# Block sums of a product's weights: from vector instructions to accumulating transfers

## The chip, the cores and the metric

The kernel runs on one core of a Trainium2 chip. The metric is the device time of one execution in microseconds, the median of three runs. A profile is one further execution with the hardware profiler; its span is the time from the first instruction to the last, which is a little less than that execution's own time. All instructions are in one program with five engine queues: PE multiplies matrices, ACT applies functions and copies, DVE and POOL do elementwise work, SP issues transfers. POOL can issue transfers too, in its own queue.

## The reference, cut to what matters

One residual layer on x of 512 tokens by 1024 channels, in f32. After a normalisation, one wide projection gives the inputs of two attention mixers, of their gates and of two output gates:

```
h = rmsnorm(x, norm_g)
(q_lat, c_kv, k_rope, z_a, q_b, k_b, v_b, z_b,
 q_idx, k_idx, w_idx, gate_a, gate_b) = split(h @ w_in)
...
merged = sigmoid(gate_a) * (y_a @ w_o_a) + sigmoid(gate_b) * (y_b @ w_o_b)
x = x + merged @ w_out
return rmsnorm(x, final_g)
```

The change touches the part of `h @ w_in` that gives `v_b` (1024 to 512) and six of the eight 128-channel tiles of `gate_b` (1024 to 1024), and there only how the same products are formed.

## The kernel before, in words

**Three-fold products.** Every f32 operand is held as a rounded part and a remainder (`hi`, `lo`), and each product is three matmuls (`mm3`, issued at L390): hi by hi, hi by lo, lo by hi. A weight tile comes from DRAM by a transfer of SP (L417) into one of four load buffers (`raw`, 128 x 1024 f32). ACT copies it to `hi` (L292), and DVE (L318) or POOL (L320) subtracts to get `lo` (`lo_part`). So ACT and one of DVE and POOL each spend one instruction on every 128 x 512 of weights before PE can use it.

**Seven products for eight.** For `v_b` (`values2`) and for three pairs of gate tiles (`proj2`: tiles 0 and 1, 2 and 3, 4 and 5 of `gate_b`) the product is cut into two by two blocks and formed with seven block products in place of eight, in Winograd's manner. That needs four block sums on the weights' side of each, made in `prep`, four sums per input tile, made once in `input_sums`, and seven steps that collect the block products from PSUM, in `seven`. The first tile of a pair holds the blocks b11 and b21 in its buffer, the second b12 and b22. Before the change `prep` of a pair forms t3 = b22 - b12 in a slot of its own, then b12 - b11 over b12, t3 + b11 over b11, and b21 minus that over b21. Each is one elementwise instruction of 128 x 512 on DVE (L318) or POOL (L320). The block products are taken in the order 1, 6, 2, 7, 5, 4, 3. Products 1, 2, 4 multiply plain blocks of h (`s_h` in the profile), 6, 7, 5, 3 sums of them (`s_hs`). Each of a pair's seven is twelve matmuls of 256 columns; each of `v_b`'s is twenty-four. The bank of product 6 is read once and then has product 7 added into it.

**A planner sets the order.** The program is written as threads (generators), each yielding one step after another. When the kernel is built, `Flow.run` keeps a clock for each engine, prices each step by a written formula, always emits the step that can start first by these clocks (with small terms for priority), and, where a step may go to either of two engines, takes the one that it expects to finish sooner. The resulting order of each engine's instructions is fixed: on the chip every engine runs its list in order and waits where an operand isn't there. A changed price or a new step can therefore move instructions anywhere behind it. `soon(...)` marks steps for which POOL is offered at its plain price.

**Jobs.** The weight tiles are jobs in a fixed list. Around the change it reads: the four tiles of `v_b` (`VB`), `GB0 GB1`, `sb2` (a key and a query tile), `zb1`, `GB2 GB3`, `sb3`, `zb2`, `GB4 GB5`, a tile of `w_out`, `zb3` and so on. One thread (`fetcher`) loads them in that order as load buffers come free. One thread (`splitter`) prepares them in that order, and for `VB` and the pairs it runs the whole `prep` before it goes on to the next job; slots for split weights are limited (`PCAP` 10, `WCAP` 8). One thread (`multiplier`) emits their matmuls in that order. The attention heads are threads beside it and fill in between.

**Transfers from POOL.** `pool_dma` (L421) and `pool_dma_out` (L437) issue transfers from POOL's queue. Both are used in the first 75 us only: constants, the rotary tables, and eight copies for the indexer. The planner prices the issue at 1.03 us of POOL.

Of the kernel before, what the change touches and what calls it, by code (L numbers as in the profile page):

```python
# [14 lines left out]
ALU = mybir.AluOpType  # L15
# [227 lines left out]
def tile_block(ctx: ExitStack, tc: tile.TileContext, a: dict, out: bass.AP, bias_dram: bass.AP):  # L243
# [40 lines left out]
    def bufs(*vs):  # L284
        return [v.buf for v in vs if isinstance(v, View)]
# [24 lines left out]
    def soon(step):  # L310
        step.pbias = 0.0
        return step
# [86 lines left out]
    def cut(pair, sl):  # L399
        return pair[0][:, sl], pair[1][:, sl]  # L400
# [17 lines left out]

    def pool_dma(dst, src):
        s = src.ap if isinstance(src, View) else src  # L420
        step = Step([("POOL", 1.03, lambda: nc.gpsimd.dma_start(dst.ap, s))], bufs(dst), bufs(src))  # L421
        step.moves = 4.0 * dst.n * dst.ap.shape[0] / 360000
        yield step

    def act_dma(dst, src):
        step = Step([("ACT", 0.06, lambda: nc.scalar.dma_start(dst.ap, src))], bufs(dst), [])
# [7 lines left out]
        return View(v.buf, bass.AP(a.tensor, a.offset + (col[1] - 1) * col[0], [row, [-col[0], col[1]]]))  # L434

    def pool_dma_out(dst, src):
        step = Step([("POOL", 1.03, lambda: nc.gpsimd.dma_start(dst, src.ap))], [], bufs(src))  # L437
        step.moves = 4.0 * src.n * src.ap.shape[0] / 360000
        yield step

# [405 lines left out]
    def splitter():  # L846
        for job in jobs:
            yield Until(lambda: job.raw is not None)
            if job.prep:
                if job.body:  # L850
                    yield from job.prep(job)
                else:
                    spawn(job.prep(job), 9)
                continue
            for p, w in enumerate(job.widths):
                o = sum(job.widths[:p])
                yield from split_w(job.raw[:, o : o + w], w, job.parts, p, job.cls, job.cap, p == len(job.widths) - 1)

    def multiplier():
        for job in jobs:  # L860
# [23 lines left out]

    hs = {}

    def input_sums():

        yield Until(lambda: sums_due[0] in done)
        for k in range(4):
            f = []
            for i in (k, k + 4):
                t = yield slot("tmp", TCAP)
                yield soon(tt(t.all.f, hT[i][0].all.f, hT[i][1].all.f, ALU.add, BOTH))
                f.append(t)
            x, y = (t.all.f for t in f)
            yield soon(tt(x[:, HI], x[:, LO], x[:, HI], ALU.subtract, BOTH))
            yield soon(tt(y[:, HI], y[:, HI], x[:, HI], ALU.subtract, BOTH))  # L900
            yield soon(tt(x[:, LO], y[:, HI], x[:, LO], ALU.add, BOTH))
            yield soon(tt(y[:, LO], y[:, LO], y[:, HI], ALU.subtract, BOTH))
            for i in range(2):
                hi = yield slot("hs")
                lo = yield slot("hs")
                yield act(hi.all, f[i].all.f)
                yield soon(lo_part(lo.all, f[i].all.f, hi.all))
                put(f[i])
                hs[k, i] = (hi, lo)

    def side(n, k):

        if n in (1, 2, 4):
            return cut(hT[k if n == 1 else k + 4], HI if n == 4 else LO)
        return cut(hs[k, n in (3, 6)], HI if n in (6, 7) else LO)

    def proj2(first, second):

        parts, raws = {}, []

        def hold(job):
            raws.append(job.raw)
            yield Until(lambda: True)

        def split_t(n, x):
            hi = yield slot("w", PCAP)
            lo = yield slot("w", PCAP)
# [48 lines left out]
        Job(a[first[0]][first[1]], [512, 512], None, prep=hold)  # L976
        Job(a[second[0]][second[1]], [512, 512], body, prep=prep)

    def seven(times, part, c11, c21, c12, c22, end):

        sums = set()

        def take(key, step, release=None):
            yield step
            if release:
                put(release)
            sums.add(key)
            if len(sums) == 7:
                end()

        def add(dst, ps, y):
            return tt(dst, part(ps), y, ALU.add)
# [16 lines left out]
        spawn(take("c22", add(c22, z, c21)), 0)  # L1009
# [5 lines left out]
        spawn(take("c12", add(c12, z, c12), z), 0)  # L1015

    def pair_done():
        hT_done()
# [6 lines left out]
    def values2():  # L1025
# [18 lines left out]

        def prep(job):
            yield Until(lambda: len(raws) == 3)
            raws.append(job.raw)
            b11, b21, b12, b22 = ([r[:, :S], r[:, S:]] for r in raws)

            def op(dst, x, y, how):  # L1050
                for i in range(2):
                    yield soon(tt(dst[i], x[i], y[i], how, BOTH))

            yield from split_t(1, b11)
            t = []
            for _ in range(2):
                t.append((yield slot("wsum")))
            t3 = [x.all.f for x in t]
            yield from op(t3, b22, b12, ALU.subtract)
            yield from op(b12, b12, b11, ALU.subtract)  # L1060
            yield from op(b11, t3, b11, ALU.add)
            yield from split_t(6, b11)
            yield from split_t(2, b21)
            yield from split_t(7, t3)
            put(*t)
            yield from split_t(5, b12, raws[2])
            yield from op(b21, b21, b11, ALU.subtract)
            put(raws[0])
            yield from split_t(4, b21, raws[1])
            yield from split_t(3, b22, raws[3])  # L1070

        def times(n, ps, more=False):
            for k in range(4):
# [940 lines left out]
```

## Time and profile before

| what | value |
|---|---|
| median of three runs | 434.74 us (434.64 to 435.3) |
| the profiled execution's own time | 435.09 us |
| its span | 433.3 us |
| granted clock of PE | 0.996 |
| busy: PE, DVE, ACT, POOL | 420.7, 382.5, 263.1, 131.7 us |
| transfers | 66.28 MB, mean 153 GB/s |

The span leaves out 1.79 us of the execution's own time (435.09 - 433.3). A busy share is the time in which an engine had an instruction in work; matmuls overlap one another in the pipeline, so a PE that is always busy needn't run at its best rate. In a timeline a row gives start, duration, engine, line, operation, what is written and read, the shape, how many, and in brackets the idle time before it with what ended that. In the groups the columns are the count, the shortest, median and longest duration in ns, and the first and last start. Windows give the busy time of each engine within each stretch, with the number of instructions.

### The profile page before, as it was taken

The numbers are of one execution on the slowest core, as the hardware profiler recorded it, in microseconds if no ns is written. First come the engines' busy times: TensorE is split into PE (matmuls) and PEld (weight loads), VectorE is DVE, ScalarE is ACT, GpSimd is POOL, SyncE is SP. The second block draws the span as 40 slices with busy tenths as digits, with TensorE's granted clock in tenths as the row PEclk, the third lists the DMA queues.
The fourth block names the chain that finished last, engine by engine and source line by source line (L and its number), as shares of the span: only waits on it lengthen the run. The fifth ranks groups of instructions, "written<-read, shape, count | busy, mean of one in ns | idle before, by whom it ended". The sixth has DMA issues, their size and how long they took to land.

```text
span 433.3 us, 7175 instructions
## 1 busy us (share of the span) xinstructions
PE 420.7 (97%) x2303; PEld 364.6 (84%) x2303; DVE 382.5 (88%) x842; ACT 263.1 (61%) x590; POOL 131.7 (30%) x152
## 2 busy tenths in 40 slices
PE   8999999899999999999999999999999999999994
PEld 5899968789888888788899988998898888888883
DVE  4599599999999999999978898989699847999995
ACT  5985785746473556655655668585389524346624
POOL 2255877444556558720000001021010001001452
PEclk9999999999999999999999999999999999999998
DMA  8973335564517451184335424525342696528405
GB/s 257 393 236 108 75 109 179 127 199 104 159 50 194 129 145 48 52 240 134 98 86 195 147 97 107 131 86 199 88 146 74 240 342 220 191 102 290 147 2 194
DMA packets 30277, 66.28 MB, mean 153 GB/s; under 512 B 4648, under 2 KB 5176, under 8 KB 30240
## 3 DMA queue, kind: packets, MB, share of 16 engines
q1 hardware_dynamic: 29264, 64.34, 48.4%
q0 software_dynamic: 832, 1.35, 1.2%
q8 instruction: 18, 0.29, 0.3%
q14 instruction: 19, 0.16, 0.1%
q10 hardware_dynamic: 144, 0.13, 0.1%
HBM read 50.49 MB, written 4.21 MB: 126 GB/s over the span
## 4 chain that ended last, share of the span: by engine, by line
PE 51%; DVE 26%; issue 8%; ACT 5%; POOL 4%; DMA 4%; SPq 1%; POOLq 0%; DVEq 0%; ACTq 0%
PE ps L390 47%; DVE mask L789 3%; DVE sm L788 3%; PE ps L407 3%; DVE sm L1430 2%; DVE s_mg L318 2%; DVE s_wo L318 2%; ACT s_w L292 2%; DVE s_ph L318 1%; DMA raw<-w_kvl 1%; SPq L417 1%; DVE s_pair L318 1%; DVE s_wsum L318 1%; DMA s_op<-s_op 1%; ACT junk L301 1%
## 5 line engine op out<-in xcount | busy, mean ns | idle before, releaser
L390 PE MATMUL ps<-s_h,s_w 128*128 128x512 f32 (+1 forms) x732 | 169.1, 378 | 0.0
L390 PEld LDWEIGHTS ps<-s_h,s_w 128*128 128x128 f32 x732 | 128.5, 188 | 22.4 <-issue 0.3
L292 ACT CAST s_w<-raw 128x512 fp32r<-128x512 f32 (+3 forms) x124 | 71.2, 591 | 21.7 <-DVE raw L318 9.6
L320 POOL TENSOR_TENSOR s_w<-raw,s_w 128x512 fp32r<-128x512 f32 (+2 forms) x41 | 50.7, 1244 | 88.2 <-ACT s_w L292 70.5
L318 DVE TENSOR_TENSOR s_w<-raw,s_w 128x512 fp32r<-128x512 f32 (+2 forms) x83 | 55.1, 679 | 10.6 <-ACT s_w L292 9.2
L390 PE MATMUL ps<-s_ys,s_w 128*128 128x512 f32 x192 | 43.7, 389 | 0.0
L390 PEld LDWEIGHTS ps<-s_ys,s_w 128*128 128x128 f32 x192 | 36.0, 188 | 7.5
L390 PE MATMUL ps<-s_wo,s_mg 128*128 128x512 f32 (+1 forms) x156 | 33.0, 373 | 0.0
L390 PE MATMUL ps<-s_w,s_xg 128*128 128x328 f32 (+1 forms) x192 | 32.4, 323 | 0.0
L390 PEld LDWEIGHTS ps<-s_w,s_xg 128*128 128x128 f32 x192 | 31.5, 188 | 0.8 <-DVE s_w L318 0.2
L390 PEld LDWEIGHTS ps<-s_wo,s_mg 128*128 128x128 f32 x156 | 27.6, 188 | 5.2
L301 ACT ACTIVATE s_p<-s_p,sm 128x384 f32<-128x384 f32 (+3 forms) x50 | 26.1, 546 | 5.3 <-DVE sm L1528 5.0
L789 DVE MATCH_REPLACE8 mask<-sm,mask 128x256 f32<-128x256 f32 (+2 forms) x48 | 25.8, 542 | 0.0
L788 DVE MAX8 sm<-mask 128x8 f32<-128x256 f32 (+2 forms) x48 | 25.5, 549 | 0.4 <-POOL mask L444 0.2
L301 ACT ACTIVATE s_p<-ps,sm 128x128 f32<-128x128 f32 (+3 forms) x32 | 16.7, 526 | 14.5 <-DVE sm L1430 14.3
L407 PE MATMUL ps<-ident,s_p 128*128 128x128 f32 x160 | 22.7, 272 | 0.0
L351 POOL TENSOR_SCALAR s_p<-s_p,sm 128x128 f32<-128x128 f32 (+3 forms) x32 | 17.1, 540 | 17.7 <-DVE sm L1407 17.3
L390 PE MATMUL ps<-s_lat,s_w 128*128 128x512 f32 x78 | 21.5, 398 | 0.0
L390 PE MATMUL ps<-s_hs,s_w 128*128 128x256 f32 x144 | 20.6, 286 | 0.5 <-DVE s_pair L318 0.5
L407 PEld LDWEIGHTS ps<-ident,s_p 128*128 128x128 f32 x160 | 18.9, 140 | 2.1
L320 POOL TENSOR_TENSOR s_p<-s_bias,mask 128x128 f32<-128x128 f32 (+2 forms) x3 | 2.6, 867 | 57.7 <-DMA s_bias<-bias_scratch 57.7
L390 PEld LDWEIGHTS ps<-s_hs,s_w 128*128 128x128 f32 x144 | 18.7, 190 | 1.0 <-DVE s_pair L318 0.7
(198 smaller groups left out, 809.5 us busy)
## 6 DMA issues: line engine op xcount, KB each, us to landing
raw<-w_out SPq DMA_DIRECT2D x18, 512.0 KB, 4.2
s_op<-s_op SPq DMA_DIRECT2D x36, 128.0 KB, 2.4
raw<-w_ga SPq DMA_DIRECT2D x8, 512.0 KB
raw<-w_gb SPq DMA_DIRECT2D x8, 512.0 KB, 4.0
raw<-w_o SPq DMA_DIRECT2D x16, 256.0 KB, 3.3
s_x<-xT SPq DMA_DIRECT2D x8, 256.0 KB, 5.7
s_xn<-x SPq DMA_DIRECT2D x8, 256.0 KB, 5.5
bias_scratch<-s_sig SPq DMA_DIRECT2D x8, 256.0 KB, 3.6
```

The lines of the kernel that those rows point to most:

```text
L292: nc.scalar.copy(dst.ap, src.ap)
L301: nc.scalar.activation(dst.ap, src.ap, func, **kw)
L318: opts.append(("DVE", 0.07 + 0.00104 * x.n, lambda: nc.vector.tensor_tensor(dst.ap, x.ap, y.ap, op=op)))
L320: opts.append(("POOL", 0.15 + 0.0021 * x.n, lambda: nc.gpsimd.tensor_tensor(dst.ap, x.ap, y.ap, op=op)))
L351: lambda: nc.gpsimd.tensor_scalar(dst.ap, x.ap, s.ap, 1.0, ALU.mult, ALU.mult)))
L390: nc.tensor.matmul(ps.ap, l.ap, r.ap, start=start and i == 0, stop=stop and i == len(pairs) - 1, skip_group_check=more)
L407: nc.tensor.transpose(d.ap, s.ap, ident.tile)
L417: return Step([("SP", n / 360000.0, lambda: nc.sync.dma_start(d, s))], bufs(dst), bufs(src))
L788: yield Step([("DVE", t, lambda: nc.vector.max(m8.tile, work.tile))], [m8], [work])
L789: yield Step([("DVE", t, lambda: nc.vector.match_replace(work.tile, m8.tile, work.tile, MARK))], [work], [m8])
L1430: yield Step([("DVE", 0.07 + 0.00104 * n, lambda: nc.vector.tensor_reduce(mx.tile[:, 1:2], ps.tile[:, :n], op=ALU.max, axis=AX.X, negate=T ...
```

## The change

- In `proj2` all four block sums of a pair become transfers with an adding write: POOL issues a transfer that reads a weight block from DRAM again and adds it to what stands in the load buffer (`add_dma`). The buffer that held b12 runs through b12 + b22, then + b11, then + b21; the one that held b11 becomes b11 + b12. Each addition into the first buffer has to wait until the split of the sum before has been made from it, since that split reads the same buffer. The slot for t3 is no longer needed.
- [...] The products are now taken in the order 1, 7, 2, 6, 5, 4, 3; product 6 has a bank of its own (`w`), and nothing is added into 7's bank (`y`).
- `values2` keeps its sums on DVE and POOL, as plain additions, and forms the first of them ahead of the split of b11. The rest of its order follows the new one.
- The planner's price of issuing a transfer on POOL goes from 1.03 to 0.55 us, in `pool_dma` and `pool_dma_out` too. The adding transfer is priced at 0.55 us of POOL and at twice the bytes of a plain one.
- `BYDMA` is false for every job and `FROMD` is false, so the new branch in `splitter` and `low_by_dma` are never entered.

```
 def pool_dma(dst, src):
-    step = Step([("POOL", 1.03, lambda: nc.gpsimd.dma_start(dst.ap, s))], bufs(dst), bufs(src))
+    step = Step([("POOL", 0.55, lambda: nc.gpsimd.dma_start(dst.ap, s))], bufs(dst), bufs(src))
...
+def add_dma(dst, src):
+    s = src.ap if isinstance(src, View) else src
+    step = Step([("POOL", 0.55, lambda: nc.gpsimd.dma_start(dst.ap, s, accum_op=ALU.add))], bufs(dst), bufs(dst, src))
+    step.moves = ADDC * dst.n * dst.ap.shape[0] / 360000
+    return step
...
 (proj2, prep)
-    raws.append(job.raw)
     b11, b21 = raws[0][:, :S], raws[0][:, S:]
-    b12, b22 = raws[1][:, :S], raws[1][:, S:]
+    x, b22 = job.raw[:, :S], job.raw[:, S:]
+    yield add_dma(x, dram(second, 1))
     yield from split_t(1, b11)
-    t = yield slot("wsum")
-    t3 = t.all.f
-    yield soon(tt(t3, b22, b12, ALU.subtract, BOTH))
-    yield soon(tt(b12, b12, b11, ALU.subtract, BOTH))
-    yield soon(tt(b11, t3, b11, ALU.add, BOTH))
-    yield from split_t(6, b11)
+    yield add_dma(b11, dram(second, 0))
+    yield from split_t(7, x)
+    yield add_dma(x, dram(first, 0))
     yield from split_t(2, b21)
-    yield from split_t(7, t3)
-    put(t)
-    yield from split_t(5, b12)
-    yield soon(tt(b21, b21, b11, ALU.subtract, BOTH))
-    yield from split_t(4, b21)
+    yield from split_t(6, x)
+    yield add_dma(x, dram(first, 1))
+    yield from split_t(5, b11)
     put(raws[0])
     yield from split_t(3, b22)
-    put(raws[1])
+    yield from split_t(4, x)
+    put(job.raw)
...
 (seven)
-    yield from times(6, y)
+    yield from times(7, y)
     yield Until(lambda: "1" in sums)
-    spawn(take("u2", add(c12, y, c22)), 0)
     yield from times(2, x, True)
     spawn(take("c11", act(c11, part(x)), x), 0)
+    w = yield bank("mm")
+    yield from times(6, w)
+    spawn(take("u2", add(c12, w, c22), w), 0)
     yield Until(lambda: "u2" in sums)
-    yield from times(7, y, True)
-    spawn(take("u3", add(c21, y, c22), y), 0)
+    spawn(take("u3", add(c21, y, c12), y), 0)
...
+ADDC = 8.0
+FROMD = False
+BYDMA = lambda job, p: False
```

More of the change, by code (lines that the diff above doesn't have):

```diff
@@ L856, in splitter @@
                 o = sum(job.widths[:p])
-                yield from split_w(job.raw[:, o : o + w], w, job.parts, p, job.cls, job.cap, p == len(job.widths) - 1)
+                last = p == len(job.widths) - 1
+                if not BYDMA(job, p):
+                    yield from split_w(job.raw[:, o : o + w], w, job.parts, p, job.cls, job.cap, last)
+                    continue
+                raw = job.raw[:, o : o + w]
+                hi = yield slot(job.cls, job.cap)
+                lo = yield slot(job.cls, job.cap)
+                yield act(hi[:, :w], raw)
+                if FROMD:
+                    if last:
+                        put(raw.buf)
+                    raw = job.src[:, o : o + w]
+                yield from low_by_dma(lo[:, :w], raw, hi[:, :w])
+                if last and not FROMD:
+                    put(raw.buf)
+                job.parts[p] = (hi, lo)
     def multiplier():
@@ L898, in input_sums @@
             x, y = (t.all.f for t in f)
+            yield soon(tt(y[:, HI], x[:, HI], y[:, HI], ALU.subtract, BOTH))
             yield soon(tt(x[:, HI], x[:, LO], x[:, HI], ALU.subtract, BOTH))
-            yield soon(tt(y[:, HI], y[:, HI], x[:, HI], ALU.subtract, BOTH))
-            yield soon(tt(x[:, LO], y[:, HI], x[:, LO], ALU.add, BOTH))
-            yield soon(tt(y[:, LO], y[:, LO], y[:, HI], ALU.subtract, BOTH))
+            yield soon(tt(x[:, LO], y[:, HI], x[:, LO], ALU.subtract, BOTH))
+            yield soon(tt(y[:, LO], y[:, LO], x[:, LO], ALU.add, BOTH))
             for i in range(2):
@@ L914, in side @@
             return cut(hT[k if n == 1 else k + 4], HI if n == 4 else LO)
-        return cut(hs[k, n in (3, 6)], HI if n in (6, 7) else LO)
+        return cut(hs[k, n in (3, 5)], HI if n in (5, 7) else LO)
     def proj2(first, second):
@@ L989, in take, with add @@
                 end()
-        def add(dst, ps, y):
-            return tt(dst, part(ps), y, ALU.add)
+        def add(dst, ps, y, op=ALU.add):
+            return tt(dst, part(ps), y, op)
         x = yield bank("mm")
@@ L1008, in seven @@
         yield Until(lambda: "u3" in sums)
-        spawn(take("c22", add(c22, z, c21)), 0)
+        spawn(take("c22", add(c22, z, c21, ALU.subtract)), 0)
         v = yield bank("mm")
@@ L1014, in seven @@
         yield from times(3, z, True)
-        spawn(take("c12", add(c12, z, c12), z), 0)
+        spawn(take("c12", add(c12, z, c12, ALU.subtract), z), 0)
     def pair_done():
@@ L1046, in prep, with op @@
             yield Until(lambda: len(raws) == 3)
-            raws.append(job.raw)
-            b11, b21, b12, b22 = ([r[:, :S], r[:, S:]] for r in raws)
-            def op(dst, x, y, how):
+            b11, b21, x, b22 = ([r[:, :S], r[:, S:]] for r in raws + [job.raw])
+            def op(dst, x, y):
                 for i in range(2):
-                    yield soon(tt(dst[i], x[i], y[i], how, BOTH))
-            yield from split_t(1, b11)
+                    yield soon(tt(dst[i], x[i], y[i], ALU.add, BOTH))
             t = []
@@ L1057, in prep @@
                 t.append((yield slot("wsum")))
[L1058 to L1061, printed above, removed]
-            yield from split_t(6, b11)
[L1063 to L1067, printed above, removed]
+            t3 = [u.all.f for u in t]
+            yield from op(t3, x, b22)
+            yield from split_t(1, b11)
+            yield from split_t(7, t3)
+            yield from op(x, x, b11)
+            yield from op(b11, t3, b11)
+            put(*t)
+            yield from split_t(2, b21)
+            yield from split_t(6, b11)
+            yield from op(b21, b21, b11)
             put(raws[0])
+            yield from split_t(5, x, raws[2])
             yield from split_t(4, b21, raws[1])
-            yield from split_t(3, b22, raws[3])
+            yield from split_t(3, b22, job.raw)
         def times(n, ps, more=False):
```

7 lines of the change are left out of this document (6 added, 1 removed).

## The prediction, on record before the result

> **What bounds the kernel now.** I read the page first, then a table of windows, then the timeline of PE. The page's first part gives the busy times:
>
> ```profile
> PE 420.7 (97%) x2303; PEld 364.6 (84%) x2303; DVE 382.5 (88%) x842; ACT 263.1 (61%) x590; POOL 131.7 (30%) x152
> ```
>
> The change takes work from DVE, which is 88% busy. PE is 97% busy, but a busy PE needn't be a fast one, so this row alone can't say which of the two sets the time. The windows say where each is full (length, then busy time of PE, PEld, DVE, ACT, POOL):
>
> ```profile
> 40.00:60.00 20.00, 18.93 (x106) 16.52 (x105) 14.30 (x19) 14.12 (x32) 16.36 (x20) 1.00 0.31 84
> 60.00:80.00 20.00, 18.49 (x90) 14.75 (x89) 18.88 (x29) 13.70 (x31) 13.30 (x15) 1.00 0.42 123
> 172.00:210.00 38.00, 37.59 (x182) 31.14 (x182) 37.50 (x83) 22.97 (x51) 12.34 (x12) 1.00 0.43 123
> 210.00:240.00 30.00, 30.00 (x218) 28.50 (x218) 24.92 (x41) 15.42 (x30) 0.00 (x0) 1.00 0.47 135
> 240.00:300.00 60.00, 59.50 (x385) 54.25 (x384) 54.56 (x138) 41.60 (x98) 6.21 (x5) 1.00 0.43 126
> 300.00:370.00 70.00, 69.97 (x369) 60.24 (x367) 55.23 (x112) 41.00 (x85) 2.60 (x2) 1.00 0.56 186
> 390.00:410.00 20.00, 20.00 (x90) 16.57 (x89) 20.00 (x40) 12.70 (x27) 4.35 (x3) 1.00 0.69 236
> 420.00:433.30 13.30, 7.04 (x42) 6.05 (x41) 8.84 (x24) 5.36 (x12) 2.74 (x4) 0.86 0.43 158
> ```
>
> Between 210 and 370, where `v_b` and all pairs are multiplied, PE is idle for 0.53 us of 160 and DVE for 25.29. The idle time of PE lies at 40 to 80 (1.07 + 1.51 = 2.58 us) and behind its last matmuls (6.26). Is the busy PE at its rate? Two stretches of 512-column matmuls, far apart, answer it:
>
> ```profile
> 177.90 22.64 PE L390 MATMUL ps<-s_h,s_w 128*128 128x512 f32 x99
> 200.38 0.64 PE L390 MATMUL ps<-s_op,qhi 128*128 128x256 f32 x4
> ...
> 364.79 23.73 PE L390 MATMUL ps<-s_ys,s_w 128*128 128x512 f32 x104
> 388.36 33.01 PE L390 MATMUL ps<-s_wo,s_mg 128*128 128x512 f32 x156
> ```
>
> From start to start, 99 matmuls take 22.48 us and 104 take 23.57: 227 ns each in both. The clock is full in every window but the last. A PE held up by others wouldn't keep one rate to half a nanosecond. So in those stretches PE runs at its rate, and **the number of matmuls sets the time**. The chain of waits seems to say something else:
>
> ```profile
> PE 51%; DVE 26%; issue 8%; ACT 5%; POOL 4%; DMA 4%; SPq 1%; POOLq 0%; DVEq 0%; ACTq 0%
> ```
>
> But it follows the last wait back, and where both are full, as at 390 to 410, it can run through either. PE lacks no time there, so shorter work on DVE would be followed by the same matmuls.
>
> [...]
>
> **The change part by part.** *Matmuls.* Seven products of twelve matmuls stay in each pair, seven of twenty-four in `v_b`. 0 us.
>
> *Sums taken away.* Four in each of three pairs, twelve in all. Their rows, three by their tile within the pairs' stretch, and one that POOL made:
>
> ```profile
> L318 DVE TENSOR_TENSOR s_wsum<-raw x3: 684/685/687, 232.3 to 299.4; 128x512 f32<-128x512 f32 x3
> 268.80 1.30 POOL L320 TENSOR_TENSOR raw<-s_wsum,raw 128x512 f32<-128x512 f32 x1 [18.28 <-ACT s_ph L292]
> ```
>
> Eleven by 0.685 is 7.5 us of DVE and 1.3 of POOL, all beside PE at its rate. I cost this at 0: cover for the missing work isn't the question, since PE is what is late next. If it were all on the path it would be worth 7.5 us (a rival below).
>
> *Twelve adding transfers.* The trace has no such transfer. From both sides, the time from issue to landing (median us, last column):
>
> ```profile
> s_qs<-s_th POOLq DMA_DIRECT2D x8, 64.0 KB, 2.0
> raw<-w_o SPq DMA_DIRECT2D x16, 256.0 KB, 3.3
> raw<-w_gb SPq DMA_DIRECT2D x8, 512.0 KB, 4.0
> ropes<-ropes POOLq DMA_DIRECT2D x1, 256.0 KB, 6.4
> ```
>
> 2.0 us is a quarter of the size, copied within the chip. 6.4 us is the right size from POOL's queue, but among the first loads of the program. An addition reads 256 KB from DRAM, and reads and writes 256 KB in the buffer, so its traffic is nearest to the 512 KB row. I take 4.0 us and 0.5 for POOL's issue (rows below): 4.5 us, with 2.0 and 6.4 as ends. POOL itself loses 12 x 0.5 us, and holds while it waits for the buffer; behind it stand at most the five POOL instructions of 240 to 300 (6.21 us), which the planner can give to DVE.
>
> [...]
>
> *The chain of three.* This is where the change can cost. Each addition into the second buffer waits for the split of the sum before: a copy on ACT,
>
> ```profile
> L292 ACT CAST s_w<-raw x30: 602/620/635, 227.8 to 301.7; 128x512 fp32r<-128x512 f32 x30
> ```
>
> a remainder of the same shape as the sums (0.69), and hand-overs, which I estimate at 0.3: about 1.6 us. The chain is add, split 7, add, split 6, add, split 4. PE takes the products in a fixed order; the places in the first pair now:
>
> ```profile
> 238.60 1.60 PE L390 MATMUL ps<-s_h,s_w 128*128 128x256 f32 x12
> 240.04 1.60 PE L390 MATMUL ps<-s_hs,s_w 128*128 128x256 f32 x12
> ...
> 244.90 0.96 PE L390 MATMUL ps<-s_hs,s_w 128*128 128x256 f32 x6
> ...
> 248.04 1.60 PE L390 MATMUL ps<-s_hs,s_w 128*128 128x256 f32 x12
> 249.48 1.60 PE L390 MATMUL ps<-s_h,s_w 128*128 128x256 f32 x12
> 251.58 1.70 PE L390 MATMUL ps<-s_hs,s_w 128*128 128x256 f32 x12 [0.50 <-DVE s_pair L318]
> 253.12 2.24 PE L390 MATMUL ps<-s_h,s_w 128*128 128x512 f32 x9
> ```
>
> and the first sum of each pair starts, in order, at
>
> ```profile
> 232.27 0.69 DVE L318 TENSOR_TENSOR s_wsum<-raw 128x512 f32<-128x512 f32 x1
> ...
> 267.25 0.69 DVE L318 TENSOR_TENSOR s_wsum<-raw 128x512 f32<-128x512 f32 x1
> ...
> 299.44 0.68 DVE L318 TENSOR_TENSOR s_wsum<-raw 128x512 f32<-128x512 f32 x1
> ...
> 287.77 1.31 PE L390 MATMUL ps<-s_h,s_w 128*128 128x256 f32 x9
> ...
> 321.21 1.31 PE L390 MATMUL ps<-s_h,s_w 128*128 128x256 f32 x9
> ```
>
> First pair, from 232.3 in steps of 4.5 + 1.6: product 7 is ready at 238.4 (second place, 240.0), 6 at 244.5 (fourth, 244.9), 4 at 250.6 (sixth, 249.5). So it is 1.1 us late at its end, and the 0.5 that PE waits there now falls into that: **+0.6 us**. The next job's split comes behind it, 252.2 against 253.1, in time. Second pair: 4 is ready at 267.3 + 18.3 = 285.6, its place is 287.8. Third: 317.7 against 321.2. Both hidden, by 2.2 and 3.5 us. At 6.4 us the steps are 8.0, the chain 24.0: late by 6.8, 3.5 and 2.2, **12.5 us** in all. At 2.0 it is 0. Each microsecond on an addition is three on the chain, so this term turns on that one size.
>
> *PSUM.* Product 6 now has its own bank, so at most three are held (x, y, w), which the class allows; z has to wait for the copy out of x, which runs beside the twelve matmuls of 6 (1.44 us from start to start in the rows above, against a copy of half of 0.62). One read ahead of an adding product goes. Between nothing and -0.5, the one wait of PE in that stretch; taken as 0, being counted above.
>
> *`values2` and `input_sums`.* The same instructions in another order. The last remainder of `v_b`'s first split and its first product are at
>
> ```profile
> 212.60 0.69 DVE L318 TENSOR_TENSOR s_w<-raw,s_w 128x512 fp32r<-128x512 f32 x1 [0.31 <-ACT s_w L292]
> ...
> 218.45 3.04 PE L390 MATMUL ps<-s_w,s_h 128*128 128x256 f32 x24
> ```
>
> so 5.2 us lie between them, and the split is pushed behind two sums, 1.4 us. 0, and at most +1.4.
>
> *The lower price of a POOL issue.* The planner now believes each issue in the first 75 us 0.48 us shorter. The rows of the most frequent ones say that the new price is right:
>
> ```profile
> L421 POOL DMA_DIRECT2D s_qs<-s_th x8: 514/534/608, 43.5 to 73.5; - x8
> L421 POOL DMA_DIRECT2D qhi<-s_oh x4: 504/519/536, 29.4 to 30.9; - x4
> ```
>
> But nothing is issued faster on the chip by this; only the order may change. PE's 2.58 idle us at 40 to 80 can fill or grow. The chain of waits runs through POOL there:
>
> ```profile
> 39.14 1.01 POOL sm L368
> 40.15 1.60 POOL s_th L320
> 41.74 1.52 POOL s_latraw L351 x2
> ```
>
> With the eight issues from 43 to 74 the planner gets 3.8 us of POOL back and can move two or three remainders from DVE (1.3 us each on POOL, like the sum above). But `s_th` takes 1.60 us where the formula for 512 columns says 0.15 + 0.0021 x 512 = 1.23, so the old price also made up for steps that are priced too low. From -2.6 to +2.6; I take 0, having no reason for a sign.
>
> [...] The eight issues of 43 to 74 kept to 0.51 to 0.61 us beside a DVE that is full to 94% at 60 to 80; no run here shows it for an adding one.
>
> **Sum.** 0 + 0.6 + 0 + 0 = +0.6 us on 435.09, the profiled execution's own time, so 435.7; against the median, 434.74 + 0.6 = **435.3 us**. 0.2% of 434.74 is 0.87 us, about what a measurement of this kernel can tell from no change: 433.87 to 435.61.
>
> **The rivals.**
>
> *A, the forecast:* PE is the bound before and after, the additions hide but for about a microsecond: 434.2 to 436.2. For it the equal rates. 0.38, of which 0.04 faster, 0.21 the same, 0.13 slower.
>
> *B, the additions land late:* at 5.5 us or more PE waits for product 4 of the first pair, since its list is fixed: at 5.5 the chain is 21.3 us, 253.6 against 249.5, +4.1, or 438.8; at 6.4 +12.5, or 447.2. It decides from 4.1 us on, where 3 x 5.7 = 17.2 uses up the 17.2 us from 232.3 to 249.5. For it the 6.4 row and three waits in line; against it the 4.0 of `w_gb`, and that the planner may put attention work in the gap. 0.24, slower.
>
> *C, the right price fills the early gap:* -1 to -2.6 us by the windows at 40 to 80, and -0.5 in the first pair: 431.6 to 433.7. For it the measured 0.53. 0.26, faster.
>
> *D, the early order gets worse:* POOL is loaded up to its true limit, the chain at 39 to 44 is late, PE's gap doubles: +1 to +2.6, 435.7 to 437.3. For it the 1.60 against 1.23. 0.09, slower.
>
> *E, DVE is the bound after all:* the 7.5 us go from the end, 427.2. For it the chain's 26% and DVE at 20.00 of 20.00 at 390; against it 227 ns everywhere, and that the third pair's last products, soon after 321, lie more than 60 us ahead of that stretch. [...] 0.03, faster.
>
> Faster 0.04 + 0.26 + 0.03 = 0.33; the same 0.21; slower 0.13 + 0.24 + 0.09 = 0.46. The range takes A, D, C down to 432.0 and B up to 441.5, about an addition of 6 us; E, the ends of B and of C stay out, some 0.15. A's own range is 434.2 to 436.2.
>
> **What would show it.** Twelve accumulating POOL issues near 0.5 us, and landing near 4 us; above 5 speaks for B, and then the timeline of PE shows idle time ahead of product 6 or 4 of the first pair. PE's matmuls stay 2303 and at 227 ns. DVE's busy time is lower by about 7 us and the span isn't. The windows at 40 to 80 tell C from D: PE's idle time there against 2.58 us. I am wrong altogether if the order changes so much elsewhere that PE idles by microseconds in a stretch where it now has none, behind 370 above all, where DVE is full too and has nothing to spare.

## The result, and the profile after

The kernel with the change takes **451.24 us** (median of 4, 449.47 to 452.28), the one before 434.69 beside it: a ratio of 1.037 (95% interval 1.034 to 1.041), 16.6 us slower. It lies outside the predicted range. The profiled execution took 452.28 us, with a span of 450.5 (before 433.3) and a granted clock of 0.987 (0.996).

The page of the profile after: busy times, the chain of waits, the costliest group that is new, and the adding transfers (last column: median us from issue to landing).

```profile
PE 427.4 (95%) x2303; PEld 368.7 (82%) x2303; DVE 378.4 (84%) x823; ACT 265.0 (59%) x596; POOL 144.6 (32%) x165
...
PE 44%; DVE 22%; DMA 14%; ACT 11%; issue 6%; POOL 2%; SPq 0%; POOLq 0%; DVEq 0%; ACTq 0%
...
L428 POOL DMA_DIRECT2D raw<-w_gb x12 | 10.5, 901 | 70.3 <-DVE s_w L318 32.0
...
raw<-w_gb POOLq DMA_DIRECT2D x12, 256.0 KB, 5.9
```

PE has the same 2303 matmuls. Its idle time in the span goes from 12.6 us (433.3 - 420.7) to 23.1 (450.5 - 427.4), so 10.5 of the 17.2 us of span are waits of PE. The other 6.7 are in its busy time, 420.7 to 427.4. By the granted clock some 4 of them are matmuls that ran slower (an estimate from the two spans: 450.5 x 0.013 less 433.3 x 0.004 is 4.1); what the rest is was not traced. DVE is busy for 4.1 us less. Transfers were 4% of the chain and are 14%.

Where it was lost is read from the timeline of PE: the start of the first group of twelve `s_hs` matmuls of each pair, and of the first `s_ys` group. The stretches between them, before and after:

| stretch | before | after | lost |
|---|---|---|---|
| start to the first pair | 240.04 | 244.99 | 4.95 |
| first pair to second | 38.44 | 42.49 | 4.05 |
| second to third | 33.70 | 39.26 | 5.56 |
| third to first `s_ys` | 32.66 | 35.29 | 2.63 |
| from there to the end of the span | 88.46 | 88.47 | 0.01 |

The windows after (length, then busy time of PE, PEld, DVE, ACT, POOL, then the granted clock):

```profile
40.00:60.00 20.00, 16.98 (x96) 15.30 (x95) 15.18 (x20) 13.50 (x30) 16.99 (x22) 1.00 0.38 110
60.00:80.00 20.00, 20.00 (x100) 16.22 (x99) 17.87 (x31) 15.55 (x35) 13.48 (x15) 1.00 0.45 127
80.00:100.00 20.00, 18.98 (x98) 16.10 (x96) 20.00 (x54) 10.36 (x27) 9.11 (x14) 1.00 0.54 157
100.00:120.00 20.00, 19.00 (x106) 16.79 (x107) 18.91 (x55) 11.08 (x27) 9.63 (x12) 0.91 0.50 126
240.00:260.00 20.00, 17.58 (x130) 16.56 (x130) 14.53 (x22) 10.79 (x21) 4.67 (x4) 0.95 0.50 115
260.00:280.00 20.00, 20.00 (x109) 17.35 (x109) 16.36 (x48) 15.38 (x38) 2.38 (x3) 0.96 0.50 135
280.00:300.00 20.00, 16.82 (x98) 15.16 (x97) 12.19 (x34) 7.54 (x21) 1.07 (x2) 0.91 0.70 150
320.00:340.00 20.00, 18.05 (x122) 16.30 (x121) 12.59 (x38) 11.61 (x29) 2.15 (x2) 1.00 0.63 159
340.00:390.00 50.00, 50.00 (x238) 41.75 (x237) 39.69 (x70) 30.00 (x58) 1.29 (x1) 1.00 0.61 210
```

and one of them before:

```profile
100.00:120.00 20.00, 20.00 (x119) 17.80 (x118) 19.84 (x61) 11.56 (x29) 9.19 (x12) 1.00 0.54 143
```

After the change PE has idle time in six of them, and the clock is below 1.00 in four: 100 to 120, and the three from 240 to 300. At 40 to 80 the idle time is 3.02 us, where it was 2.58; at 80 to 120 it is 2.02, where it was 0.19. So most of the early loss of 4.95 us arises at 80 to 120: 1.8 us more of idle time and, by the clock of 0.91, about 1.8 of slower running (an estimate, 20 x 0.09). From 340 to 390 PE is full at the full clock, and the last stretch of the table is as long as before. What PE waited for, grouped (us in total, times, longest):

```profile
PE ps L390 <- DMA qhi<-s_op: 2.8, 1, 2.8
PE ps L778 <- DVE s_qs L318: 2.6, 1, 2.6
PE ps L407 <- POOL s_p L351: 2.0, 2, 1.6
PE ps L407 <- ACT s_p L301: 1.7, 3, 1.1
```

The second is there in the kernel before too (at L766), with 1.0 us; the others are new at this length. None names an adding transfer. The first pair shows why: the chain of waits there, with start and length,

```profile
237.24 5.30 DMA raw<-w_gb
...
242.69 0.63 ACT s_w L292
...
243.35 0.70 DVE s_w L318
...
244.33 4.03 DMA raw<-w_gb
...
250.03 5.50 DMA raw<-w_gb
...
255.55 0.63 ACT s_w L292
...
256.25 1.56 POOL s_w L320
```

and what PE does at its end:

```profile
252.98 1.95 PE L390 MATMUL ps<-s_hs,s_w 128*128 128x256 f32 x15
256.22 0.50 PE L390 MATMUL ps<-s_h,s_w 128*128 128x256 f32 x2 [1.29 <-ACT s_w L292]
257.85 2.25 PE L390 MATMUL ps<-s_h,s_w 128*128 128x256 f32 x10 [1.13 <-POOL s_w L320]
259.90 2.35 PE L390 MATMUL ps<-s_hs,s_w 128*128 128x256 f32 x12
262.08 2.23 PE L390 MATMUL ps<-s_h,s_w 128*128 128x512 f32 x9
```

Three additions, each behind the split of the sum before, end at the remainder for product 4, and PE waits for it twice. The wait is booked to ACT and POOL, which only come last in line; the chain shows the transfer behind them. From issue to landing the three take 5.30, 4.03 and 5.50 us. Twelve matmuls of product 3 then take 2.18 us from start to start (259.90 to 262.08), where twelve took 1.44 before.

In the second pair the wait is at another place. SP's queue and PE:

```profile
289.51 0.34 SPq L417 DMA_DIRECT2D raw<-w_zb  x1
289.94 0.63 SPq L417 DMA_DIRECT2D qhi<-s_op  x1
```

```profile
295.87 2.72 PE L390 MATMUL ps<-s_op,qhi 128*128 128x256 f32 x8 [2.78 <-DMA qhi<-s_op]
```

PE waits 2.78 us for a query tile of the attention. Its transfer stands in SP's list behind the load of `w_zb`, and that load needs a load buffer, which is free only when a sum has been split from it. The chain of waits names the steps:

```profile
279.35 8.11 DMA raw<-w_gb
...
287.54 0.63 ACT s_w L292
...
288.80 0.69 DVE s_w L318
289.51 0.34 SPq L417
...
289.94 5.88 DMA qhi<-s_op
```

So an addition that landed late delayed the splits behind it on ACT and DVE, these the buffer, the buffer a load, and the load a transfer that has nothing to do with the pair. This is read from one trace; no experiment took this path alone out.

### The profile page after: what moved, and what is told of

Its sections match the earlier page's. It is cut to its first block, busy times and chain, and to the rows that moved or that the text cites. A ratio compares the mean times of both kernels' runs of the same rounds, so it can differ in the third digit from the quotient of the medians.

```text
span 450.5 us, 7217 instructions
## 1 busy us (share of the span) xinstructions
PE 427.4 (95%) x2303; PEld 368.7 (82%) x2303; DVE 378.4 (84%) x823; ACT 265.0 (59%) x596; POOL 144.6 (32%) x165
## 3 DMA queue, kind: packets, MB, share of 16 engines
HBM read 53.63 MB, written 4.21 MB: 128 GB/s over the span
## 4 chain that ended last, share of the span: by engine, by line
PE 44%; DVE 22%; DMA 14%; ACT 11%; issue 6%; POOL 2%; SPq 0%; POOLq 0%; DVEq 0%; ACTq 0%
PE ps L390 38%; DMA raw<-w_gb 9%; ACT s_p L301 4%; DVE s_w L318 4%; PE ps L407 3%; DVE mask L801 3%; DVE s_tmp L318 3%; ACT s_w L292 2%; DVE sm L800 2%; DMA s_op<-s_op 1%; ACT junk L301 1%; DMA qhi<-s_op 1%; DMA raw<-w_kvl 1%; DVE mask L329 1%; DVE raw L318 1%
## 5 line engine op out<-in xcount | busy, mean ns | idle before, releaser
L390 PE MATMUL ps<-s_h,s_w 128*128 128x512 f32 (+1 forms) x732 | 171.2, 381 | 2.8 <-ACT s_w L292 1.3
L292 ACT CAST s_w<-raw 128x512 fp32r<-128x512 f32 (+3 forms) x127 | 73.1, 592 | 40.2 <-DMA raw<-w_gb 25.6
L320 POOL TENSOR_TENSOR s_w<-raw,s_w 128x512 fp32r<-128x512 f32 (+2 forms) x42 | 54.2, 1298 | 116.9 <-ACT s_w L292 67.0
L318 DVE TENSOR_TENSOR s_w<-raw,s_w 128x512 fp32r<-128x512 f32 (+2 forms) x85 | 60.2, 724 | 23.7 <-ACT s_w L292 23.5
L428 POOL DMA_DIRECT2D raw<-w_gb x12 | 10.5, 901 | 70.3 <-DVE s_w L318 32.0
L301 ACT ACTIVATE s_p<-s_p,sm 128x256 f32<-128x256 f32 (+3 forms) x56 | 29.4, 551 | 3.8 <-DVE sm L1562 3.8
L407 PE MATMUL ps<-ident,s_p 128*128 128x128 f32 x160 | 24.6, 279 | 3.8 <-POOL s_p L351 2.0
L351 POOL TENSOR_SCALAR s_p<-s_p,sm 128x128 f32<-128x128 f32 (+3 forms) x32 | 17.2, 542 | 19.1 <-DVE sm L1441 18.4
L390 PE MATMUL ps<-s_hs,s_w 128*128 128x256 f32 x144 | 21.8, 294 | 0.0
L390 PEld LDWEIGHTS ps<-s_hs,s_w 128*128 128x128 f32 x144 | 20.1, 202 | 0.3
```

The source lines that it names most:

```text
L292: nc.scalar.copy(dst.ap, src.ap)
L301: nc.scalar.activation(dst.ap, src.ap, func, **kw)
L318: opts.append(("DVE", 0.07 + 0.00104 * x.n, lambda: nc.vector.tensor_tensor(dst.ap, x.ap, y.ap, op=op)))
L320: opts.append(("POOL", 0.15 + 0.0021 * x.n, lambda: nc.gpsimd.tensor_tensor(dst.ap, x.ap, y.ap, op=op)))
L351: lambda: nc.gpsimd.tensor_scalar(dst.ap, x.ap, s.ap, 1.0, ALU.mult, ALU.mult)))
L390: nc.tensor.matmul(ps.ap, l.ap, r.ap, start=start and i == 0, stop=stop and i == len(pairs) - 1, skip_group_check=more)
```

## The experiments

Theory after the result: the loss has two sources, the lower price (early) and the additions (in the pairs). Rivals: the price costs nothing and the new transfers hold up all the rest; or the new order of products does it by itself.

**1. The price alone.** The kernel before with

```diff
-        step = Step([("POOL", 1.03, lambda: nc.gpsimd.dma_start(dst.ap, s))], bufs(dst), bufs(src))
+        step = Step([("POOL", 0.55, lambda: nc.gpsimd.dma_start(dst.ap, s))], bufs(dst), bufs(src))
```

and the same in `pool_dma_out`.

> The kernel before with one edit: the planner's price of a POOL issue is 0.55 in place of 1.03 us, and nothing else. After loses 4.95 us ahead of the first matmul of v_b (218.45 to 223.40) and about 12 us in the three pairs. Theory: the early part is the price's, by a changed order in the first 120 us, so this kernel takes 434.7 + 5 = 439.7 us (438 to 441). Rival: the price is harmless (433.9 to 435.6) and the early loss comes back from the new order of the sums through the planner.

441.47 us, ratio 1.015 (1.012 to 1.019): +6.9. The four runs spread from 439.26 us at a granted clock of 0.999 to 442.88 at 0.988, so what this price costs depends on how far the clock falls in a run; the profiled run is the longest. The early loss is there without any adding transfer: the first pair starts at 245.59 in it, 5.55 us late. POOL has 160 instructions in place of 152 and 13.3 us more work (145.0 against 131.7), and DVE none less (384.5 against 382.5). POOL's timeline and PE's show one of the places:

```profile
99.74 1.27 POOL L320 TENSOR_TENSOR s_w<-raw,s_w 128x512 fp32r<-128x512 f32 x1 [0.17 <-ACT s_w L292]
101.00 1.73 POOL L351 TENSOR_SCALAR s_p<-s_p,sm 128x256 f32<-128x256 f32 x3
```

```profile
102.09 0.33 PE L407 MATMUL ps<-ident,s_p 128*128 128x128 f32 x1 [1.70 <-POOL s_p L351]
...
103.39 2.91 PE L390 MATMUL ps<-s_lat,s_w 128*128 128x512 f32 x6
```

The `s_p` that PE needs next stands on POOL behind a remainder of 1.27 us. The six 512-column matmuls behind the wait take 2.91 us by their row; at 227 ns they would take about 1.4. The expected 439.7 was missed by 1.8 us; the wait for it comes late, at 339 (experiment 8).

**2. The change with the old price** for plain transfers (1.03), adding ones still at 0.55.

> After with the old price of 1.03 us for the plain transfers of POOL; the adding transfers, their price of 0.55 and the new signs stay. Theory: the early 5 us go and the pairs' 12 stay, 446.3 us (445 to 448). Rival, that the early loss is not the price's: 451.2.

448.32 us, ratio 1.032 (1.027 to 1.036). The first pair starts at 241.47, so 3.5 us of the early loss are gone; the stretches of the pairs stay as long (43.19, 39.26, 35.86). The expectation was 2 us too low: the gain in total is 2.9. (The stretches are those of the profiled run, at 451.17 us the longest of the four.)

**3. The change with vector sums.** All of the change except that `prep` makes its four sums with vector instructions. The sums stay additions, where three of four were differences before, and the signs that go with this, in the input's sums and in two collecting steps, stay too:

```diff
-            yield add_dma(x, dram(second, 1))
+            t = yield slot("wsum")
+            t3 = t.all.f
+            yield soon(tt(t3, x, b22, ALU.add, BOTH))
...
-            yield add_dma(b11, dram(second, 0))
+            yield soon(tt(x, x, b11, ALU.add, BOTH))
```

> After with the pairs' sums as four additions on DVE or POOL again, in the order that values2 now has; new signs, own bank for product 6 and the price of 0.55 stay. Theory, that the adding transfers make PE wait in the pairs: the 12 us go, 439.7 us (438 to 441). Rival, that the new order of products and the third bank are what PE waits for: 449 to 452.

444.38 us, ratio 1.023 (1.021 to 1.024). So the adding transfers cost 6.9 of the 16.6 us. But 2.9 us stay over the price alone, which neither theory had: the new signs and order cost something themselves.

**4. The transfers without the addition.** The same instruction lists as after, with `accum_op` left out. The kernel leaves out the block sums.

```diff
-        step = Step([("POOL", 0.55, lambda: nc.gpsimd.dma_start(dst.ap, s, accum_op=ALU.add))], bufs(dst), bufs(dst, src))
+        step = Step([("POOL", 0.55, lambda: nc.gpsimd.dma_start(dst.ap, s))], bufs(dst), bufs(dst, src))
```

> After with the twelve adding transfers issued as plain ones from the same queue at the same places (each overwrites the block in place of adding to it, so the block sums are left out). The instruction lists are those of after. If the addition itself is what lands late (5.9 us median against 3.3 for 256 KB from SP), landing falls to 3.3 to 4 us, each chain gets 6 to 8 us shorter, and the pairs' loss falls from 12 to 3 to 5 us: 442 to 445 us. If it is POOL's queue and the waits ahead of the issue, landing stays over 5 us and the time at 449 to 452.

441.34 us, ratio 1.014 (1.013 to 1.016): 9.9 us faster than after, by the addition alone, and a little under the expected range. The issue group and the landing:

```profile
L428 POOL DMA_DIRECT2D raw<-w_gb x12 | 6.5, 543 | 67.8 <-DVE s_w L318 30.6
...
raw<-w_gb POOLq DMA_DIRECT2D x12, 256.0 KB, 4.0
```

The same 256 KB land in 4.0 us plain and in 5.9 adding, and take 0.54 us of POOL to issue against 0.90. With a plain landing the stretches of the pairs are 39.18, 36.40 and 32.41 us (42.49, 39.26 and 35.29 with the addition), so 0.7 and 2.7 longer and 0.3 shorter than before. In the first pair PE still waits 0.64 us for the remainder of product 4 (256.34, `<-POOL s_w`), in the second 1.21 for the query tile (291.20).

**5. The new signs and order alone**: experiment 3 with the old price, so neither source of the theory is in it.

> The new signs, the new order of products, the own bank for product 6 and the new order in values2, but the pairs' sums on DVE or POOL and the old price of 1.03 us. What is left of the change is only its algebra. Theory, that the price and the adding transfers are the whole loss: 434.6 us (433.5 to 436). Rival, that the new order has a cost of its own, as the 2.9 us between this form and the form before at the price of 0.55 (444.4 against 441.5) may say: 437.5 us.

440.73 us, ratio 1.013 (1.011 to 1.015). I had expected no change, and the reordering by itself costs 5.8 us. The stretches of the pairs are 39.12, 33.84 and 36.67 (before 38.44, 33.70, 32.66): 4.0 of it lie behind the third pair. PE and DVE there:

```profile
335.62 15.07 PE L390 MATMUL ps<-s_h,s_w 128*128 128x512 f32 x58 [2.23 <-DVE s_w L318]
```

```profile
331.08 2.48 DVE L329 SCALAR_TENSOR_TENSOR s_ys<-s_y,s_ys 128x512 fp32r<-128x512 f32 x4
...
334.28 0.69 DVE L329 SCALAR_TENSOR_TENSOR s_ys<-s_y,s_ys 128x512 fp32r<-128x512 f32 x1
334.88 2.49 DVE L318 TENSOR_TENSOR s_w<-raw,s_w 128x512 fp32r<-128x512 f32 x4
```

PE waits for the remainder of the next gate tile, which begins at 334.88. DVE has first made five splits of `s_ys`, which PE needs at 350.54 only. ACT's copy for that remainder stands behind `s_ys` steps as well (331.71).

**6. The change with true prices**: experiment 2, with an addition priced at 0.9 us of POOL and 2.0 us later in landing, so that the planner knows what experiment 4 measured.

```diff
-                    end = self.dma + 1.0
+                    end = self.dma + 1.0 + step.late
...
-        step = Step([("POOL", 0.55, lambda: nc.gpsimd.dma_start(dst.ap, s, accum_op=ALU.add))], bufs(dst), bufs(dst, src))
+        step = Step([("POOL", 0.9, lambda: nc.gpsimd.dma_start(dst.ap, s, accum_op=ALU.add))], bufs(dst), bufs(dst, src))
+        step.late = 2.0
```

> After with the old price for plain transfers, and with the adding transfers priced as measured: 0.9 us of POOL and 2.0 us later landing, so that the planner believes in some 6 us from issue to end. Theory, that PE waits because its fixed list was made for additions that land 2 us too early: the planner fills the gaps with attention work, and 448.3 falls to 438 to 442. Rival, that the chain itself is too long for what stands ahead of PE (one splitter, four load buffers), whatever the planner knows: 445 to 449.

450.53 us, ratio 1.035 (1.032 to 1.037), above the rival's range too. The theory that the planner only lacked the right price falls. The first pair's stretch is now 45.45 us, the second and third together 73.44 (75.12 in experiment 2): the loss is moved, not removed. The planner did put attention work into the first pair, but PE then waits for that: 1.07 us for DVE's `sm` (255.32) and 1.43 for ACT's `s_p` (258.68).

**7. The first addition early**: experiment 2, with the first addition of each pair in a thread of its own, ahead of the splitter's arrival. It takes one of three out of the chain.

```diff
-            yield add_dma(x, dram(second, 1))
+            yield Until(lambda: begun)
...
+        job2 = Job(a[second[0]][second[1]], [512, 512], body, prep=prep)
+        begun = []
...
+        def first_add():
+            yield Until(lambda: job2.raw is not None)
+            yield add_dma(job2.raw[:, :S], dram(second, 1))
+            begun.append(1)
+
+        spawn(first_add(), 9)
```

> The kernel after with the old price for plain transfers (448.3 us), with the first adding transfer of each pair issued by a thread of its own as soon as the pair's second tile is there, and not when the splitter reaches the pair. Theory: the chain of three additions, counted from the splitter's arrival, sets the loss at the pairs; with one of the three out of it, it is some 6 us shorter in each pair, and the time falls to 441 to 445 us. Rival: the queue of POOL or the tile's late arrival holds the first addition anyway: 447 to 449.

444.67 us, ratio 1.023 (1.018 to 1.027), 3.7 us less than experiment 2. The first pair's stretch is 39.12 and the second's 35.74, 4.1 and 3.5 us shorter, where 6 was expected; the third's is 1.7 longer (37.55). So a shorter chain does shorten the first two pairs. In the first pair the two additions left in the chain, with the splits between them, take 11.1 us up to the last remainder (240.09 to 251.17), against 11.6 in experiment 2 (241.78 to 253.38), so not all of the gain need be the addition that was moved; why it is shorter was not tried.

**8. The weights first**, in three kernels. In `y_gate` the last step (the split of `s_ys`) becomes a thread at priority 9.5 instead of 8:

```diff
-        yield is_done("pairs")
-        hi = yield slot("ys")
...
-        ysplit[br, j] = (hi, lo)
+        def cut_y():
+            yield is_done("pairs")
+            hi = yield slot("ys")
...
+            ysplit[br, j] = (hi, lo)
+
+        spawn(cut_y(), 9.5)
```

In experiment 5:

> The kernel with the new signs and order alone (vector sums, old price, 440.7 us) with one edit: the last step of each y_gate is a thread of its own at priority 9.5 instead of 8, so that behind the pairs VectorE first makes the remainders of the next gate tile and then the splits of s_ys. The lists up to the third pair are the same. Theory: of the 6.0 us that this algebra costs, some 4 are the one wait of 2.23 us for s_w at 335.6 and the slow stretch behind it, and 1.7 stand before the third pair. Then 436.4 us (435.8 to 437.5). Rival: VectorE is late there in sum, whatever its order, and the wait only moves to another tile: 439.5 to 441.

In the kernel before:

> The kernel before with the same edit (the splits of s_ys behind the next gate tile's weights). TensorE waits for neither there, so the order of the two has nothing to give: 434.3 to 435.3 us by the theory that the wait belongs to the new algebra's list. If the edit by itself shortens the end, under 434.

In experiment 1:

> The kernel before with the price 0.55 (441.5 us) and the same edit. Of its 6.9 us, 5.4 stand before the third pair's first product, and the rest holds the wait of 2.24 us for s_w at 339.3. Theory: only the rest goes, 439.2 us (438.5 to 440.2). Rival, the wait moves on: 441 to 442.

With the new algebra: 437.04 us, ratio 1.005 (1.003 to 1.006), against 440.73. In the kernel before: 434.41, ratio 0.999 (0.998 to 1.001), nothing. With the price: 438.07, ratio 1.007 (1.005 to 1.009), against 441.47, a little under its expected range. The wait of the new algebra is gone, and nothing takes its place; PE and DVE of the first of the three:

```profile
332.49 14.47 PE L390 MATMUL ps<-s_h,s_w 128*128 128x512 f32 x63
```

```profile
328.18 0.68 DVE L318 TENSOR_TENSOR s_w<-raw,s_w 128x512 fp32r<-128x512 f32 x1
```

The remainder is made at 328.18, and PE runs through its 63 matmuls in 14.31 us (332.49 to 346.80), 227 ns each. The third stretch is 32.49 us with the new algebra and 32.51 with the price, against 32.66 before: both kernels had lost time behind the third pair by this one order of steps. ACT's copy for the remainder comes earlier too (327.01).

**9. What an idle PE costs.** The kernel before, with one wait put into PE's list near 333 us: two extra matmuls, the second of which waits for a small transfer of POOL. Then the same with 24 dummy matmuls between the two, so that PE is busy while it would wait.

```diff
+        yield extra(gapt)
+        yield Step([("POOL", 0.0, lambda: nc.gpsimd.dma_start(gapt.tile, a["ident"][:, :64]))], [gapt], [])
+        for _ in range(fill):
+            yield extra(gapz)
+        yield extra(gapt)
```

> The kernel before with one wait of PE put into its full stretch near 330 us: a small matmul, a 32 KB transfer that may only start behind it, and a second small matmul that waits for the transfer. All other lists stay as they are. The two matmuls are 0.4 us, the wait 3 to 4. If an idle PE costs only its idle time: 434.6 + 4 = 438.5. If PE runs slowly for some time behind a wait of that length, as the rows behind waits over 1.6 us in after seem to show (six 512-column matmuls in 2.6 us in place of 1.4): 1.3 to 2.5 us more, about 440.5.

> The same with 24 small matmuls (about 5.2 us of work that nobody needs) between the two, so that PE is never idle while the transfer lands. If it is idleness that slows PE afterwards, no matmul behind it is slow, and the time is 434.6 + 5.2 + 0.4 = 440.2 us. If the slow stretch has another cause, the rows behind it are slow here too and the time is 441.5 or more.

438.91 us (ratio 1.009, 1.007 to 1.011) and 440.87 (1.014, 1.012 to 1.016). The totals lie between the expectations and don't decide; the rows behind the wait do. Empty and filled:

```profile
335.55 0.39 PE L874 MATMUL ps<-gapz,gapt 128*128 128x512 bf16 x1 [2.27 <-DMA gapt<-ident]
335.58 12.85 PE L390 MATMUL ps<-s_h,s_w 128*128 128x512 f32 x48
348.27 1.98 PE L390 MATMUL ps<-s_ys,s_w 128*128 128x512 f32 x8
```

```profile
338.82 11.24 PE L390 MATMUL ps<-s_h,s_w 128*128 128x512 f32 x48
349.91 0.39 PE L390 MATMUL ps<-s_ys,s_w 128*128 128x512 f32 x1
```

The windows of 330 to 340, empty and filled:

```profile
330.00:340.00 10.00, 7.72 (x28) 5.84 (x27) 9.94 (x17) 6.62 (x13) 0.60 (x1) 0.83 0.32 111
```

```profile
330.00:340.00 10.00, 10.00 (x48) 6.07 (x47) 9.94 (x17) 7.15 (x14) 0.60 (x1) 1.00 0.30 102
```

The same 48 matmuls take 12.69 us behind 2.27 us of idle time and 11.09 behind dummy work; the granted clock is 0.83 and 1.00. So this wait cost 2.27 us and then 1.6 more.

The length of a wait alone doesn't decide this, though. In the kernel after, PE waited 2.57 us for `s_qs` (until 58.25), and the clock stayed at 1.00 from 40 to 80; in experiment 1 it waited 2.64 us at the same place (until 58.09), and the clock was 0.97 over 40 to 60 and 0.95 over 60 to 80. The first three 512-column matmuls behind that wait take 0.70 us in the kernel after (59.09 to 59.79) and 1.28 in experiment 1 (59.19 to 60.47).

## Why the prediction was wrong

**What bounds the kernel: right.** PE at its rate was the bound, and taking work from DVE gave nothing: from the first `s_ys` group to the end, where E saw its 7.5 us, the kernel after takes 88.47 us and the one before 88.46. Where PE doesn't wait it still takes 227 ns per matmul (experiment 8). Rival E falls. What I didn't draw from it: where an engine is full, a new order has only the engine's idle time to win, and any wait to lose.

**Matmuls, sums taken away: right.** 2303 before and after; the relief bought nothing. It was smaller than the 7 us I named as a sign: DVE's busy time fell by 4.1, and its remainders (`s_w<-raw,s_w`) take 60.2 us where they took 55.1.

**The twelve adding transfers: the size that failed.** I took "4.0 us and 0.5 for POOL's issue", since the traffic was "nearest to the 512 KB row". Experiment 4 shows that 4.0 is the landing of the plain transfer of this size. The addition lands in 5.9, above the 5 named as the sign for rival B, and its issue takes 0.90. Counting its traffic twice did not stand in for what an addition costs: the page after lists 256 KB for each, and 3.14 MB more read from DRAM for the twelve (53.63 against 50.49), and what an addition moves within the buffer is in no view.

**The chain of three: right in form, wrong in its sizes.** With additions the chain starts 6.3 us ahead of the pair's first product, as its first sum did before (237.24 against 243.55; 232.27 against 238.60). Product 4 is ready 14.3 us behind that product (257.85) where I had 12.0 (250.6 against 238.60), and the stretch is 4.05 us longer. Of these 2.3 us, 1.3 are the three additions (14.8 us where I had 13.5) and 1.0 the splits (5.8 where I had 4.8), the last of them with its remainder on POOL, 1.56 us in place of 0.69. "The second and third hidden by 2.2 and 3.5" failed as well: they lost 5.56 and 2.63. I looked for the loss at the pairs' own products only, but in the second pair it is a query tile that comes late, behind a load buffer in SP's list.

**Where numbers agree by luck.** With plain transfers the first pair's stretch is 0.7 us longer than before, and I had +0.6; PE does wait for product 4 there (0.64 us), but the stretch is 39.12 with vector sums too (experiment 5), where there is no added transfer. Rival B priced the pairs at 12.5 for an addition of 6.4 us, and they lost 12.2. At the 5.9 measured its sum gives 8.0 (5.3, 2.0 and 0.7), and it knows neither the query tile nor the slower clock. B had the first pair's mechanism and not the sum. Two of its figures were also too low by its own sum: at 5.5 us the second pair is late as well, by 0.8, so 439.6 and not 438.8; and at 6 us it gives 443.6, so the range's end of 441.5 stood for about 5.8.

**`values2` and `input_sums`, the new order: failed.** "The same instructions in another order. 0, and at most +1.4." Experiment 5 gives 5.8 us, and experiment 8 shows that 3.7 of them are one wait of PE, with the slow matmuls behind it, that arises 100 us behind the edit. I weighed the edit at its own place and not what the planner makes of it later.

**The lower price: failed.** "From -2.6 to +2.6; I take 0." It costs 6.9 us alone (experiment 1): 5.5 before the first pair in the profiled run, and the rest for the most part by the same wait behind the third pair, which goes with experiment 8. Rival D had the sign but neither the size nor the place: PE's idle time at 40 to 80, which it saw doubled from 2.58, is 3.02 after, and most of the early loss lies at 80 to 120. The row that said that 0.53 us is the right price was true, and so was the one beside it, `s_th` at 1.60 us against a formula of 1.23; whether the second is why the order got worse is not shown.

**A term that was missing.** Some 4 of the 17.2 us, by the granted clock, are matmuls that ran slower behind the waits. Every term of the sum priced an idle microsecond of PE at one.

**How the 16.6 us add up.** Put in one after the other: the price 6.9 (441.5), the new signs and order 2.9 more (444.4), the adding transfers 6.9 more (451.2). In another order the parts differ (the algebra alone is 5.8, and both it and the price alone include the wait behind the third pair), so the shares belong to this order; and the first has a 95% interval from 5 to 8 us. In the lists of after the addition alone is worth 9.9 (experiment 4), which is more than 6.9: with vector sums the wait behind the third pair comes back (a third stretch of 36.68 us in experiment 3, 32.41 in experiment 4). Open is why a landing took 4.0 us in one place and 8.1 in another within the same kernel, and which step of DVE first falls behind with the lower price. No kernel here is faster than the one before; the nearest, the kernel before with the weights first, can't be told from it.

## What to carry to other kernels

Where one engine is at its rate and its list is fixed, price a change by the latest operand in each list it touches, and count what stands behind that operand in the same queue, up to a hundred microseconds on; relief for another engine was worth nothing here. A transfer that adds is to be priced by a measurement of its own, and in a chain of them it counts once per link: 5.30, 4.03 and 5.50 us in the first pair. Correcting one price in a planner can cost time, 6.9 us here: what counts is the order that comes of it.

## What the runs showed of the hardware

- An adding transfer of 256 KB from DRAM into a buffer, issued by POOL, lands in 5.9 us (median of 12) and takes 0.90 us to issue; the plain one, at the same places in the same lists, 4.0 and 0.54.
- Behind 2.27 us without a matmul the granted clock was 0.83 over the window of 330 to 340, and the next 48 matmuls took 1.6 us more; with dummy matmuls in the gap the clock was 1.00. Whether a wait of that length lowers the clock varies: behind 2.57 us in the kernel after it was 1.00 from 40 to 80, behind 2.64 us at the same place in experiment 1 it was 0.97 over 40 to 60 and 0.95 over 60 to 80. Behind a wait of 1.65 us in the kernel after the clock was 0.50 from 102 to 104, and six 512-column matmuls took 2.63 us instead of about 1.4:

```profile
100.63 0.33 PE L407 MATMUL ps<-ident,s_p 128*128 128x128 f32 x1 [1.65 <-POOL s_p L351]
...
102.09 2.79 PE L390 MATMUL ps<-s_lat,s_w 128*128 128x512 f32 x6
104.72 0.50 PE L407 MATMUL ps<-ident,s_p 128*128 128x128 f32 x3
```

In the kernel before, PE waited up to 1.4 us in one piece, at 40 to 80, and the clock stayed at 1.00 there.
